# Feed-forward output products as block products: 7 of 256 columns in place of 8, with sums on VectorE and the residual in DRAM

## The chip, the cores and the metric

One NeuronCore of a Trainium2 chip runs the whole program. The metric is the device time of one execution in microseconds. The kernel is written in a Python tile language: a scheduler orders the instructions of each engine when the program is built, and each engine then works through its own queue in that order and waits on semaphores. PE is TensorE, PEld its weight loads, DVE is VectorE, ACT is ScalarE, POOL is GpSimd, and SP issues the weights' DMAs.

## The reference

A trunk of two layers works on a residual x of 512 tokens by 1024 channels, in float32. Each layer is a half feed-forward step, a mixer, and another half feed-forward step:

```
x = x + 0.5 * swiglu(rms_norm(x), w_i1, w_o1)
h = rms_norm(x); p = h @ w_in            # q/k/v of four mixers and the gates' logits
merged = sum_b sigmoid(gate_b) * (branch_b @ w_branch_b)
x = x + merged @ w_out
x = x + 0.5 * swiglu(rms_norm(x), w_i2, w_o2)

def swiglu(h, w_i, w_o):
    gate, up = jnp.split(h @ w_i, 2, axis=-1)
    return (jax.nn.silu(gate) * up) @ w_o
```

The hidden width of the feed-forward networks (FFN) is 2816, which is 22 chunks of 128. There are four FFNs, called a0, b0, a1 and b1 after their place ahead of the mixer or behind it and their layer.

## The kernel before

**Products.** Channels lie on the 128 partitions and the 512 tokens are the columns. A float32 product is made of three matmuls: weights and activations are each held as a rounded part (hi, h) and a remainder (lo, l), and `mm3` (lines 231 to 236) adds hi·h, hi·l and lo·h into one PSUM tile. The weights are the stationary operand, 128x128, loaded anew for each matmul; the activations move, 512 columns at a time.

**Weights.** `load_split` (lines 141 to 152) brings in up to four chunks of 128 columns at once: SP issues a DMA into a raw tile (three buffers), ACT copies it into hi, and DVE (in part of the mixer in turn with POOL) subtracts to get lo. `chain` does that for a row of chunks and issues their mm3.

**An FFN.** In the in stage, for each of 22 j, two chains of eight chunks make a gate and an up-projection; DVE multiplies both by the norm's scale, ACT applies silu, and the product is split into fh and fl, which all stay in SBUF. In the out stage, for each m of eight output rows, one chain of 22 chunks makes a PSUM tile, `L278` adds half of it to the residual x[m], which lies in SBUF, and the next norm squares it, sums the squares (ssq) and makes its parts xh and xl (`L188`, `L189`).

**The mixer.** After four attention branches come, for each branch and each m, a gate (three ACT steps, `L614` to `L616`) and a branch product; DVE multiplies them (`L632`) and adds them to acc[m] (`L634`). Then eight chains over mh and ml, the two parts of acc (`L1087`, `L1088`), make the output product pmo, to which the residual xr is added as it comes back from DRAM. Tiles of mh and ml are taken from rings that the mixer has used for other tiles.

What sets the order on an engine is the scheduler, by the order of the code, the buffers and `high_priority`; the mixer has its own planner, which the change leaves as it is.

Of the kernel before, what the change touches and what calls it, by code (L numbers as in the profile page):

```python
# [21 lines left out]
P = 128  # L22
D = 1024
S = 512
# [24 lines left out]
COL = 64  # L49
RING = 8192  # L50
# [44 lines left out]
def trunk_kernel(ctx: ExitStack, tc: tile.TileContext, a, out):  # L95
# [43 lines left out]
    lo_parts = dict(count=0, shared=False)  # L139

    def load_split(src, n, name):
        raw = wp.tile([P, CW], F32, tag="raw", name=f"raw{name}", bufs=3)
# [23 lines left out]
    class Norm:  # L166
        def __init__(self, l, which, name):
            self.l, self.col, self.name = l, PV[which], name
            self.xh, self.xl = [], []
            self.ssq = per.tile([P, S], F32, tag="ssq", name=f"ssq{name}")  # L170
# [12 lines left out]

        def split(self, m, xt):
            g = pv[:, self.l, self.col + m:self.col + m + 1]
            xh = per.tile([P, S], F32R, tag="xh", name=f"xh{self.name}_{m}", bufs=NK)
            xl = per.tile([P, S], F32R, tag="xl", name=f"xl{self.name}_{m}", bufs=NK)
            A.activation(xh, xt, AF.Copy, scale=g)  # L188
            V.scalar_tensor_tensor(xl, xt, g, xh.bitcast(F32), ALU.mult, ALU.subtract)  # L189
            self.xh.append(xh)  # L190
            self.xl.append(xl)
# [61 lines left out]
    def ffn(l, w_in, w_out, x, nrm, nxt, name, final, early=None):  # L253
        with tc.tile_pool(name=f"ff{name}", bufs=2, reuse_waits="tile") as fp:
            fh, fl = [], []
            for j in range(NH):
                if j == 2 and early is not None:
                    early()
                pg = mm_tile(f"pg{name}{j}")
                chain(pg, w_in[l, j, 0], nrm.xh, nrm.xl, f"g{name}{j}")  # L260
                pu = mm_tile(f"pu{name}{j}")
                chain(pu, w_in[l, j, 1], nrm.xh, nrm.xl, f"u{name}{j}")
                g = fp.tile([P, S], F32, tag="g", name=f"g{name}{j}")
                u = fp.tile([P, S], F32, tag="u", name=f"u{name}{j}")
                V.tensor_tensor(g, pg, nrm.rb, ALU.mult)
                A.activation(g, g, AF.Silu)
                V.tensor_tensor(u, pu, nrm.rb, ALU.mult)
                V.tensor_tensor(u, u, g, ALU.mult)
                h = fp.tile([P, S], F32R, tag="fh", name=f"fh{name}{j}", bufs=NH)
                lo = fp.tile([P, S], F32R, tag="fl", name=f"fl{name}{j}", bufs=NH)  # L270
                A.activation(h, u, AF.Copy)
                V.tensor_tensor(lo, u, h.bitcast(F32), ALU.subtract)
                fh.append(h)
                fl.append(lo)
            for m in range(NK):
                po = mm_tile(f"po{name}{m}")
                chain(po, w_out[l, m], fh, fl, f"o{name}{m}")
                V.scalar_tensor_tensor(x[m], po, 0.5, x[m], ALU.mult, ALU.add)  # L278
                if final:
                    (nc.sync if m == NK - 1 else nc.gpsimd).dma_start(out[m], x[m])  # L280
                else:
                    nxt.add(m, x[m], lambda n: fp.tile([P, S], F32, tag="sq", name=n, bufs=2))
# [54 lines left out]
    def mixer(l, x, nrm, nxt, xs):  # L337
        with (tc.tile_pool(name=f"mx{l}", bufs=1, reuse_waits="tile") as mp,
# [260 lines left out]
            acc = []  # L599
            wbr = {}  # L600

            def gate(b, m):
# [3 lines left out]
                if b == 0:  # L606
                    g = per.tile([P, S], F32, tag="x", name=f"acc{l}{m}", bufs=NK)
# [468 lines left out]


            lo_parts["shared"] = False
# [32 lines left out]
    with tc.tile_pool(name="first", bufs=2) as fp:  # L1111
        with tc.high_priority(offset=2 * HP):
            for m, t in enumerate(x):
                nrm.split(m, t)
# [76 lines left out]
```

## Time and profile before

| | |
|---|---|
| median of 3 runs | 2689.72 us (2689.0 to 2690.22) |
| the profiled execution's own time | 2689.76 us |
| its span | 2688.0 us |
| PE busy | 2669.4 us, 99% of the span |
| DVE, ACT, POOL busy | 55%, 49%, 12% |
| out stage of each FFN | 119.80 us |

The median is what a change is measured by. The span is what the trace covers of the profiled execution, from its first to its last instruction. The busy shares are averages over stages that differ. The out stages are the four windows from the first output matmul of an FFN to its last.

### The profile page before, as it was taken

Reading aid. Unit: us, or ns where it says so; the run is one execution under the profiler, and the core shown is the slowest. Engines: PE = TensorE matmul, PEld = TensorE weight load, DVE = VectorE, ACT = ScalarE, POOL = GpSimd, SP = SyncE. Lnnn points to the kernel's source line nnn. Section 1 sums busy time; section 2 is a strip of 40 time slices with the busy share of each in tenths; the row PEclk is TensorE's granted clock in tenths of the full one; section 3 lists DMA queues with packets and bytes.
Section 4 is the critical chain, followed back from the end, with each engine's and each line's share of the span. In section 5 each row is a group of like instructions: output and inputs, shape, how many; then the busy total and the mean of one; then the engine's idle time right before and its main releaser. Section 6 shows DMA issues by size and latency. Waiting matters only on the chain.

```text
span 2688.0 us, 36812 instructions
## 1 busy us (share of the span) xinstructions
PE 2669.4 (99%) x13054; PEld 2266.4 (84%) x13054; DVE 1486.0 (55%) x3028; ACT 1326.1 (49%) x2740; POOL 318.9 (12%) x438
## 2 busy tenths in 40 slices
PE   9999999999999999999999999999999999999999
PEld 7888889888888788888888888998888887888887
DVE  6444437777764564444354443487776646644432
ACT  4333347777665653333333333477776556433321
POOL 1000012222222200000000000222222222000000
PEclk9999999999999999999999999999999999999999
DMA  5333432222322332233322233322223223322233
GB/s 169 99 98 93 118 117 73 75 72 88 88 76 81 101 114 97 96 98 95 98 98 96 97 101 112 113 69 78 76 84 92 69 87 106 110 98 98 96 109 90
DMA packets 146488, 257.10 MB, mean 96 GB/s; under 512 B 17081, under 2 KB 47801, under 8 KB 146304
## 3 DMA queue, kind: packets, MB, share of 16 engines
q1 hardware_dynamic: 138960, 233.16, 28.1%
q0 software_dynamic: 6192, 19.50, 2.5%
q8 instruction: 102, 1.67, 0.3%
q10 hardware_dynamic: 1152, 2.10, 0.2%
q14 instruction: 82, 0.67, 0.1%
HBM read 248.31 MB, written 8.61 MB: 96 GB/s over the span
## 4 chain that ended last, share of the span: by engine, by line
PE 97%; DVE 1%; ACT 1%; issue 1%; DMA 0%; POOL 0%; ACTq 0%; POOLq 0%
PE pgl L234 4%; PE pgl L236 4%; PE pgl L235 4%; PE pga L235 3%; PE pua L234 3%; PE pua L236 3%; PE pua L235 3%; PE pga L236 3%; PE pga L234 3%; PE pob L236 3%; PE pub L234 3%; PE pgb L234 3%; PE pub L236 3%; PE poa L236 3%; PE pgb L236 3%; PE poa L235 3%
## 5 line engine op out<-in xcount | busy, mean ns | idle before, releaser
L234 PE MATMUL pgl<-xhm,higl 128*128 128x512 f32 x512 | 216.4, 423 | 0.0
L236 PE MATMUL pgl<-xhm,logl 128*128 128x512 f32 x512 | 200.9, 392 | 0.0
L235 PE MATMUL pgl<-xlm,higl 128*128 128x512 f32 x512 | 200.2, 391 | 0.0
L234 PE MATMUL pga<-xhf,higa 128*128 128x512 f32 x352 | 138.1, 392 | 3.0 <-ACT xhf L188 3.0
L150 DVE TENSOR_TENSOR loob<-rawob,hiob 128x512 fp32r<-128x512 f32 x96 | 62.0, 646 | 140.6 <-ACT hiob L147 140.6
L234 PE MATMUL pua<-xhf,hiua 128*128 128x512 f32 x352 | 137.9, 392 | 0.0
L235 PE MATMUL pga<-xlf,higa 128*128 128x512 f32 x352 | 137.4, 391 | 0.4 <-DVE xlf L189 0.4
L147 ACT ACTIVATE hiob<-rawob 128x512 fp32r<-128x512 f32 x96 | 57.3, 597 | 163.2 <-PE pob L235 138.3
L234 PE MATMUL pgb<-xhf,higb 128*128 128x512 f32 x352 | 137.8, 391 | 0.0
L235 PE MATMUL pua<-xlf,hiua 128*128 128x512 f32 x352 | 137.5, 391 | 0.0
L236 PE MATMUL pga<-xhf,loga 128*128 128x512 f32 x352 | 137.4, 390 | 0.0
L236 PE MATMUL pua<-xhf,loua 128*128 128x512 f32 x352 | 137.4, 390 | 0.0
L235 PE MATMUL pub<-xlf,hiub 128*128 128x512 f32 x352 | 137.0, 389 | 0.0
L234 PE MATMUL pub<-xhf,hiub 128*128 128x512 f32 x352 | 137.0, 389 | 0.0
L235 PE MATMUL pgb<-xlf,higb 128*128 128x512 f32 x352 | 137.0, 389 | 0.0
L236 PE MATMUL pub<-xhf,loub 128*128 128x512 f32 x352 | 137.0, 389 | 0.0
L235 PE MATMUL pob<-flb,hiob 128*128 128x512 f32 x352 | 136.9, 389 | 0.0
L234 PE MATMUL pob<-fhb,hiob 128*128 128x512 f32 x352 | 136.9, 389 | 0.0
L234 PE MATMUL poa<-fha,hioa 128*128 128x512 f32 x352 | 136.9, 389 | 0.0
L236 PE MATMUL poa<-fha,looa 128*128 128x512 f32 x352 | 136.9, 389 | 0.0
L236 PE MATMUL pgb<-xhf,logb 128*128 128x512 f32 x352 | 136.9, 389 | 0.0
L235 PE MATMUL poa<-fla,hioa 128*128 128x512 f32 x352 | 136.9, 389 | 0.0
(663 smaller groups left out, 7371.1 us busy)
## 6 DMA issues: line engine op xcount, KB each, us to landing
rawgl<-in_w_gate SPq DMA_DIRECT2D x128, 256.0 KB, 2.7
rawga<-in_f_in SPq DMA_DIRECT2D x88, 256.0 KB, 2.7
rawua<-in_f_in SPq DMA_DIRECT2D x88, 256.0 KB, 2.8
rawgb<-in_f_in SPq DMA_DIRECT2D x88, 256.0 KB, 2.7
rawub<-in_f_in SPq DMA_DIRECT2D x88, 256.0 KB, 2.8
rawoa<-in_f_out SPq DMA_DIRECT2D x80, 256.0 KB, 2.6
rawob<-in_f_out SPq DMA_DIRECT2D x80, 256.0 KB, 2.6
rawmo<-in_w_out SPq DMA_DIRECT2D x32, 256.0 KB, 2.8
```

What stands on the lines that cost most here:

```text
L147: A.activation(hi[:, :n], raw[:, :n], AF.Copy)
L150: eng.tensor_tensor(lo[:, :n], raw[:, :n], hi[:, :n].bitcast(F32), ALU.subtract)
L234: T.matmul(ps, wh, xh, start=first, stop=False)
L235: T.matmul(ps, wh, xl, start=False, stop=False)
L236: T.matmul(ps, wl, xh, start=False, stop=last)
```

## The change

In the out stage of an FFN, the chunks are divided into plain ones (14 in a0, 8 in the other three) and pairs (4 in a0, 7 in the others; `NPAIRS`). The eight output rows are taken two at a time (four `Pair`s q). The plain chunks keep their chains of 512 columns. For a pair of rows, a pair of chunks and the two halves of the columns there are four weight blocks (a, b of the first row, c, d of the second) and four blocks of activations, whose eight block products of 256 columns are replaced by seven:

- `combine`, at the end of the in stage, makes four blocks of sums and differences of activations on DVE, and splits the seven blocks that are used into fph and fpl;
- `group` handles up to four pairs of chunks at a time (four and three where there are seven): it loads the weights a, c, d and b (512 or 384 columns each), makes four sums of them on DVE (`plus`: c+d, a+c+d, a+c, a+b+c+d), splits the seven, and issues the seven products a, s, t, b, u, v, d, each into 256 columns of its own PSUM bank;
- `after` adds the seven PSUM tiles into the two rows of the residual, once the last group is done;
- the weights of w_out lie in DRAM in an order that suits these loads.

The residual isn't kept in SBUF any more: it is loaded on POOL's queue where it is needed (`x_of`) and stored there when it is new (`keep`). The parts of a norm, xh and xl, get a pool of their own, opened and closed around their use. The mixer's last part is a function of its own, `merge`, with a pool that is opened behind the mixer's; its eight mh and ml tiles come from there. The raw weights have four buffers in place of three. The making of the bias tables (`early`, in a0 alone) moves from the third j of the in stage to the second Pair of the out stage. The core of the diff:

```diff
+NPAIRS = (4, 7)
+TH = S // 2
+SLOT = dict(a=0, s=5, t=4, b=2, u=1, v=3, d=6)
...
-        raw = wp.tile([P, CW], F32, tag="raw", name=f"raw{name}", bufs=3)
+        raw = wp.tile([P, CW], F32, tag="raw", name=f"raw{name}", bufs=4)
...
+    def ffn(l, w_in, w_out, x_of, nrm, nxt, name, keep, early=None):
+        with tc.tile_pool(name=f"ff{name}", bufs=1, reuse_waits="tile") as fp:
+            plain, paired = [], []
+            npair = NPAIRS[early is None]
+            nplain = NH - 2 * npair
...
+                r2 = ip.tile([P, S], F32, tag="r", name=f"r{nm}")
+                r3 = ip.tile([P, TH], F32, tag="rs", name=f"rs{nm}")
+                V.tensor_tensor(r2[:, lo], r0[:, lo], r0[:, hi], ALU.subtract)
+                V.tensor_tensor(r2[:, hi], r1[:, hi], r2[:, lo], ALU.add)
+                V.tensor_tensor(r3, r1[:, lo], r2[:, hi], ALU.subtract)
+                V.tensor_tensor(r0[:, hi], r0[:, hi], r1[:, hi], ALU.subtract)
+                h = fp.tile([P, 7 * TH], F32R, tag="fph", name=f"fph{nm}", bufs=npair)
+                lw = fp.tile([P, 7 * TH], F32R, tag="fpl", name=f"fpl{nm}", bufs=npair)
+                for n, r in enumerate((r0, r1, r2, r3)):
+                    c = slice(n * S, n * S + (S if n < 3 else TH))
+                    split_up(h[:, c], lw[:, c], r)
+                paired.append((h, lw))
...
+                    elif j % 2 == 0:
+                        before = u
+                    else:
+                        combine(j // 2, before, u, ip)
+            nrm.close()
...
+                            xr = op.tile([P, S], F32, tag="x", name=f"x{name}{m}", bufs=4)
+                            nc.gpsimd.dma_start(xr, x_of[m])
+                            po = mm_tile(f"po{name}{m}")
+                            chain(po, w_out[l, m][:, :nplain * P], [h for h, _ in plain], [w for _, w in plain],
+                                  f"o{name}{m}")
+                            V.scalar_tensor_tensor(xr, po, 0.5, xr, ALU.mult, ALU.add)
+                            self.x.append(xr)
...
+                        def load(n, m, odd):
+                            if n == "b":
+                                t = op.tile([P, CW], F32, tag="wb", name=f"w{n}{nm}")
+                            else:
+                                t = wp.tile([P, CW], F32, tag="raw", name=f"w{n}{nm}", bufs=4)
+                            nc.sync.dma_start(t[:, :w], w_out[l, 2 * self.q + m][:, c0 + odd * w:c0 + (odd + 1) * w])
+                            return t[:, :w]
...
+                            t = op.tile([P, CW], F32, tag="ws", name=f"s{n}{nm}", bufs=3)[:, :w]
+                            with tc.high_priority(offset=HP):
+                                V.tensor_tensor(t, x, y, ALU.add)
...
+                            sl = slice(SLOT[n] * TH, (SLOT[n] + 1) * TH)
+                            for p in range(np_):
+                                fh, fl = paired[p0 + p]
+                                mm3(ps, hi, lo, p, fh[:, sl], fl[:, sl], p0 + p == 0, p0 + p == npair - 1)
+                            if last:
+                                self.after(n)
+                        a11 = load("a", 0, 0)
+                        a21 = load("c", 1, 0)
+                        product("a", a11)
+                        a22 = load("d", 1, 1)
+                        s1 = plus(1, a21, a22)
+                        s2 = plus(2, s1, a11)
+                        product("s", s2)
+                        product("t", s1)
+                        a12 = load("b", 0, 1)
+                        s3 = plus(3, a11, a21)
+                        product("b", a12)
+                        s4 = plus(4, s2, a12)
+                        product("u", s3)
+                        product("v", s4)
+                        product("d", a22)
...
+                        if n == "a":
+                            self.y = op.tile([P, S], F32, tag="y", name=f"y{nm}")
+                            A.activation(self.y[:, lo], ps, AF.Copy, scale=0.5)
+                        elif n == "s":
+                            self.up = op.tile([P, TH], F32, tag="up", name=f"up{nm}")
+                            V.scalar_tensor_tensor(self.up, ps, -0.5, self.y[:, lo], ALU.mult, ALU.add)
+                        elif n == "t":
+                            V.scalar_tensor_tensor(self.y[:, hi], ps, 0.5, self.up, ALU.mult, ALU.add)
+                            V.tensor_tensor(x1, x1, self.y, ALU.add)
+                        elif n == "b":
+                            V.scalar_tensor_tensor(x1[:, lo], ps, 0.5, x1[:, lo], ALU.mult, ALU.add)
+                        elif n == "u":
+                            self.z = op.tile([P, S], F32, tag="y", name=f"z{nm}")
+                            V.scalar_tensor_tensor(self.z[:, lo], ps, 0.5, self.up, ALU.mult, ALU.subtract)
+                            V.scalar_tensor_tensor(self.z[:, hi], self.ps["t"], -0.5, self.z[:, lo], ALU.mult, ALU.add)
+                            V.tensor_tensor(x2, x2, self.z, ALU.add)
+                        elif n == "v":
+                            V.scalar_tensor_tensor(x1[:, hi], ps, 0.5, x1[:, hi], ALU.mult, ALU.add)
+                            self.out(0)
+                        else:
+                            V.scalar_tensor_tensor(x2[:, lo], ps, 0.5, x2[:, lo], ALU.mult, ALU.add)
+                            self.out(1)
...
+                        (nc.sync if nxt is None and m == NK - 1 else nc.gpsimd).dma_start(keep[m], self.x[n])
+                        if nxt is not None:
+                            nxt.add(m, self.x[n], lambda nm: op.tile([P, S], F32, tag="sq", name=nm))
...
+                for q in range(NK // 2):
+                    if q == 1 and early is not None:
+                        early()
+                    t = Pair(q)
+                    for p0 in range(0, npair, 4):
+                        t.group(p0, min(4, npair - p0), p0 + 4 >= npair)
...
+    def merge(l, acc, nxt, xs, keep):
+        with tc.tile_pool(name=f"mo{l}", bufs=1, reuse_waits="tile") as mp:
             lo_parts["shared"] = False
             mh, ml = [], []
             for m in range(NK):
-                if m < 7:
-                    h = mp.tile([P, S], F32R, tag="oh", name=f"mh{l}{m}", bufs=7)
-                    lo = mp.tile([P, S], F32R, tag="ol", name=f"ml{l}{m}", bufs=7)
-                else:
-                    h = mp.tile([P, S], F32R, tag="st", name=f"mh{l}{m}", bufs=12)
-                    lo = mp.tile([P, S], F32R, tag="st", name=f"ml{l}{m}", bufs=12)
+                h = mp.tile([P, S], F32R, tag="mh", name=f"mh{l}{m}", bufs=NK)
+                lo = mp.tile([P, S], F32R, tag="ml", name=f"ml{l}{m}", bufs=NK)
                 A.activation(h, acc[m], AF.Copy)
                 V.tensor_tensor(lo, acc[m], h.bitcast(F32), ALU.subtract)
                 mh.append(h)
                 ml.append(lo)
-            xn = []
             for m in range(NK):
-                xr = sb_tile(f"xr{l}{m}")
+                xr = mp.tile([P, S], F32, tag="xr", name=f"xr{l}{m}", bufs=3)
                 nc.gpsimd.dma_start(xr, xs[m])
                 po = mm_tile(f"pmo{l}{m}")
                 chain(po, a["w_out"][l, m], mh, ml, f"mo{l}{m}")
-                t = per.tile([P, S], F32, tag="x", name=f"xn{l}{m}", bufs=NK)
+                t = mp.tile([P, S], F32, tag="xn", name=f"xn{l}{m}", bufs=5)
                 V.tensor_tensor(t, po, xr, ALU.add)
+                nc.gpsimd.dma_start(keep[m], t)
+                nxt.add(m, t, lambda nm: mp.tile([P, S], F32, tag="r", name=nm, bufs=6))
...
+            mixer(l, nrm, ap, acc)
+            nrm.close()
+            nxt.open()
+            merge(l, acc, nxt, xs, x)
```

On the engines the rows of the mixer, up to its last gate, stand as before; each engine has the rows of the out stages anew. PE has 13482 rows where it had 12582, which is 900 more: 3 x 252 for the three FFNs with 7 pairs and 144 for a0.

ACT at the end of layer 0's mixer, before. himo is the hi part of the weights of the output product, gt037 the gate of the last branch and row, mh05 to mh07 the copies of acc:

```order
L147 ACTIVATE himo01_0_10004<-rawmo01_0_10002 128x512
L147 ACTIVATE himo01_4_10022<-rawmo01_4_10020 128x512
L1087 ACTIVATE mh06_9945<-acc06_6134 128x512
L614 ACTIVATE gt037_9909<-gt037_9909,pv_101 128x512
L615 ACTIVATE gt037_9909<-gt037_9909,onec_94 128x512
L147 ACTIVATE himo02_0_10052<-rawmo02_0_10050 128x512
L616 ACTIVATE gt037_9909<-gt037_9909 128x512
L1087 ACTIVATE mh07_9949<-acc07_6235 128x512
L147 ACTIVATE himo02_4_10070<-rawmo02_4_10068 128x512
```

The same place after the change:

```order
L151 ACTIVATE himo01_0_10392<-rawmo01_0_10390 128x512
L151 ACTIVATE himo01_4_10410<-rawmo01_4_10408 128x512
L759 ACTIVATE gt037_10286<-gt037_10286,pv_101 128x512
L760 ACTIVATE gt037_10286<-gt037_10286,onec_94 128x512
L761 ACTIVATE gt037_10286<-gt037_10286 128x512
L1230 ACTIVATE mh00_10308<-acc00_5481 128x512
L1230 ACTIVATE mh01_10312<-acc01_5558 128x512
L1230 ACTIVATE mh02_10316<-acc02_5713 128x512
L1230 ACTIVATE mh03_10320<-acc03_5835 128x512
L1230 ACTIVATE mh04_10324<-acc04_5947 128x512
```

mh00 to mh05 stood earlier, in turn with the gates before; now all eight stand together behind the third step of gt037.

DVE at the same place after the change. pbr037 is the last branch product, ml00 and on the remainders of acc:

```order
L154 TENSOR_TENSOR lomo01_0_10393<-rawmo01_0_10390,himo01_0_10392 128x512
L154 TENSOR_TENSOR lomo01_4_10411<-rawmo01_4_10408,himo01_4_10410 128x512
L777 TENSOR_TENSOR gt037_10286<-pbr037_10291,gt037_10286 128x512
L779 TENSOR_TENSOR acc07_6612<-acc07_6612,gt037_10286 128x512
L1231 TENSOR_TENSOR ml00_10309<-acc00_5481,mh00_10308 128x512
L1231 TENSOR_TENSOR ml01_10313<-acc01_5558,mh01_10312 128x512
```

Before, ml00 to ml05 stood earlier in the same way as mh00 to mh05; now all eight stand behind the operation that finishes acc07.

PE at the same place, before and then after:

```order
L234 MATMUL pbr037_9914<-oh0D_9646,hibr034_9766 128x512
L235 MATMUL pbr037_9914<-ol0D_9647,hibr034_9766 128x512
L236 MATMUL pbr037_9914<-oh0D_9646,lobr034_9767 128x512
L234 MATMUL pmo00_9955<-mh00_9921,himo00_0_9958 128x512
L235 MATMUL pmo00_9955<-ml00_9922,himo00_0_9958 128x512
L236 MATMUL pmo00_9955<-mh00_9921,lomo00_0_9959 128x512
```

```order
L249 MATMUL pbr037_10291<-oh0D_10023,hibr034_10143 128x512
L250 MATMUL pbr037_10291<-ol0D_10024,hibr034_10143 128x512
L251 MATMUL pbr037_10291<-oh0D_10023,lobr034_10144 128x512
L249 MATMUL pmo00_10342<-mh00_10308,himo00_0_10345 128x512
L249 MATMUL pmo01_10389<-mh00_10308,himo01_0_10392 128x512
L250 MATMUL pmo00_10342<-ml00_10309,himo00_0_10345 128x512
L251 MATMUL pmo00_10342<-mh00_10308,lomo00_0_10346 128x512
L249 MATMUL pmo00_10342<-mh01_10312,himo00_0_10345 128x512
```

Nothing stands between the last branch product and the first matmul of pmo in either; after the change the chains of pmo00 and pmo01 take turns.

DVE in the out stage of b0 after the change, second Pair, where the first group (name b01_0) and the second (b01_4) meet. s1 to s4 are the sums of weights, lo with a letter the remainder of a product's weights, pob02 and pob03 the plain chains of the two rows:

```order
L355 TENSOR_TENSOR s3b01_0_13156<-wab01_0_13093,wcb01_0_13095 128x512
L336 SCALAR_TENSOR_TENSOR xb02_13013<-pob02_13015,xb02_13013 128x512
L276 TENSOR_TENSOR losb01_0_13121<-s2b01_0_13118,hisb01_0_13120 128x512
L276 TENSOR_TENSOR lotb01_0_13138<-s1b01_0_13116,hitb01_0_13137 128x512
L355 TENSOR_TENSOR s4b01_0_13175<-s2b01_0_13118,wbb01_0_13154 128x512
L355 TENSOR_TENSOR s1b01_4_13249<-wcb01_4_13230,wdb01_4_13247 128x384
L336 SCALAR_TENSOR_TENSOR xb03_13053<-pob03_13055,xb03_13053 128x512
L276 TENSOR_TENSOR lobb01_0_13159<-wbb01_0_13154,hibb01_0_13158 128x512
L276 TENSOR_TENSOR loub01_0_13178<-s3b01_0_13156,hiub01_0_13177 128x512
L355 TENSOR_TENSOR s2b01_4_13251<-s1b01_4_13249,wab01_4_13228 128x384
L276 TENSOR_TENSOR lovb01_0_13195<-s4b01_0_13175,hivb01_0_13194 128x512
L355 TENSOR_TENSOR s3b01_4_13285<-wab01_4_13228,wcb01_4_13230 128x384
```

The second group's first sum, s1b01_4, stands ahead of the split of product b of the first group. Before, this stretch of DVE held two weight splits for each four chunks of a plain chain and nothing else.

## Rows read from the trace of the kernel before

**Rows 1.** The page: busy time by engine; the chain that ended last
```profile
PE 2669.4 (99%) x13054; PEld 2266.4 (84%) x13054; DVE 1486.0 (55%) x3028; ACT 1326.1 (49%) x2740; POOL 318.9 (12%) x438
...
PE 97%; DVE 1%; ACT 1%; issue 1%; DMA 0%; POOL 0%; ACTq 0%; POOLq 0%
```

**Rows 2.** Busy time by window, the second output stage, below the view's columns
```profile
core 0: us, PE busy (x) PEld busy (x) DVE busy (x) ACT busy (x) POOL busy (x), PEclk, DMA share, GB/s
...
1229.80:1349.60 119.80, 119.80 (x530) 99.25 (x529) 46.06 (x71) 38.16 (x64) 0.00 (x0) 1.00 0.34 96
```

**Rows 3.** Timeline of PE, end of group D's projection (start us, us)
```profile
2161.53 0.36 PE L362 MATMUL pt1d<-hit1d,xhm 128*128 128x256 f32 x1
2161.73 0.28 PE L363 MATMUL pt1d<-lot1d,xhm 128*128 128x256 f32 x1
...
2161.98 0.28 PE L362 MATMUL pt1d<-hit1d,xhm 128*128 128x256 f32 x1
...
2164.37 0.28 PE L364 MATMUL pt1d<-hit1d,xlm 128*128 128x256 f32 x1
```

**Rows 4.** Single tiles (duration ns min/median/max); two rows of DVE's timeline
```profile
L150 DVE TENSOR_TENSOR looa<-rawoa,hioa x96: 424/691/694, 247.7 to 1700.3; 128x512 fp32r<-128x512 f32 x80, 128x256 fp32r<-128x256 f32 x16
...
L150 DVE TENSOR_TENSOR lot0a<-rawt0a,hit0a x16: 542/557/956, 371.3 to 443.5; 128x384 fp32r<-128x384 f32 x16
...
1405.54 0.68 DVE L150 TENSOR_TENSOR loua<-rawua,hiua 128x512 fp32r<-128x512 f32 x1
1406.14 0.68 DVE L268 TENSOR_TENSOR ua<-ua,ga 128x512 f32<-128x512 f32 x1
```

**Rows 5.** Timeline, the end; DMA issues (KB each, us to landing)
```profile
2684.16 0.69 DVE L278 SCALAR_TENSOR_TENSOR xn<-pob,xn 128x512 f32<-128x512 f32 x1 [8.87 <-PE pob L236]
...
rawoa<-in_f_out SPq DMA_DIRECT2D x80, 256.0 KB, 2.6
```

**Rows 6.** Timeline of PE, the last branch matmul and the first of pmo
```profile
945.73 0.39 PE L236 MATMUL pbr<-oh0D,lobr 128*128 128x512 f32 x1
945.96 0.39 PE L234 MATMUL pmo<-mh,himo 128*128 128x512 f32 x1
```

**Rows 7.** Timeline of ACT around the end of the mixer of layer 0
```profile
945.25 1.31 ACT L147 ACTIVATE himo<-rawmo 128x512 fp32r<-128x512 f32 x2 [2.04 <-PE pgl L235]
946.47 0.62 ACT L1087 ACTIVATE mh<-acc 128x512 fp32r<-128x512 f32 x1
946.99 0.71 ACT L614 ACTIVATE gt<-gt,pv 128x512 f32<-128x512 f32 x1
947.73 0.72 ACT L615 ACTIVATE gt<-gt,onec 128x512 f32<-128x512 f32 x1
...
949.19 0.62 ACT L616 ACTIVATE gt<-gt 128x512 f32<-128x512 f32 x1
```

**Rows 8.** Timeline of DVE there: the last gate's product and sum
```profile
949.93 0.68 DVE L632 TENSOR_TENSOR gt<-pbr,gt 128x512 f32<-128x512 f32 x1
950.64 0.69 DVE L634 TENSOR_TENSOR acc<-acc,gt 128x512 f32<-128x512 f32 x1
```

**Rows 9.** Timeline of PE at the start, and two windows (columns as above)
```profile
8.42 0.80 PE L234 MATMUL pga<-xhf,higa 128*128 128x512 f32 x1 [3.04 <-ACT xhf L188]
...
8.42:14.06 5.64, 5.23 (x12) 3.76 (x12) 5.64 (x12) 5.53 (x10) 0.00 (x0) 0.50 0.95 334
14.06:16.00 1.94, 1.94 (x10) 1.59 (x9) 1.94 (x4) 1.94 (x5) 0.00 (x0) 0.96 0.47 182
```

**Rows 10.** Two shorter idle times of PE, and the windows around them
```profile
461.62 0.63 PE L585 MATMUL pot0A<-ident,o0A 128*128 128x128 f32 x4 [1.42 <-DVE o0A L734]
...
912.28 0.51 PE L234 MATMUL pbr<-oh0D,hibr 128*128 128x512 f32 x1 [1.18 <-ACT oh0D L986]
...
459.00:462.50 3.50, 2.08 (x13) 1.58 (x12) 3.43 (x9) 3.05 (x10) 2.15 (x3) 1.00 0.21 56
909.00:915.00 6.00, 4.19 (x20) 3.05 (x19) 3.20 (x5) 3.55 (x5) 0.78 (x1) 1.00 0.28 89
```

More of the change, by code (lines that the diff above doesn't have):

```diff
@@ L169, in __init__, with open, close @@
             self.xh, self.xl = [], []
-            self.ssq = per.tile([P, S], F32, tag="ssq", name=f"ssq{name}")
+        def open(self):
+            self.pool = tc.tile_pool(name=f"x{self.name}", bufs=1, side="right", reuse_waits="tile")
+            self.xp = self.pool.__enter__()
+            self.ssq = per.tile([P, S], F32, tag="ssq", name=f"ssq{self.name}")
+        def close(self):
+            self.pool.__exit__(None, None, None)
         def add(self, m, xt, alloc):
@@ L250, in chain @@
             pass
[L253 to L280, printed above, removed]
-                else:
-                    nxt.add(m, x[m], lambda n: fp.tile([P, S], F32, tag="sq", name=n, bufs=2))
@@ L1112, in trunk_kernel @@
         with tc.high_priority(offset=2 * HP):
-            for m, t in enumerate(x):
-                nrm.split(m, t)
-        for m, t in enumerate(x):
-            nrm.square(m, t, lambda n: fp.tile([P, S], F32, tag="sq", name=n))
+            for m in range(NK):
+                nrm.split(m, x[m])
+        for m in range(NK):
+            nrm.square(m, x[m], first)
     nrm.finish()
+    x = [a["x"][m] for m in range(NK)]
     for l in range(L):
+        xs = kept(f"xs{l}")
         nxt = Norm(l, "nm", f"m_{l}")
-        ffn(l, a["f1_in"], a["f1_out"], x, nrm, nxt, f"a{l}", False, setup_bias if l == 0 else None)
+        ffn(l, a["f1_in"], a["f1_out"], x, nrm, nxt, f"a{l}", xs, setup_bias if l == 0 else None)
@@ L1121, in trunk_kernel @@
         nxt.finish_cols()
-        xs = [drm.tile([P, S], F32, name=f"xs{l}{m}") for m in range(NK)]
-        for m in range(NK):
-            nc.gpsimd.dma_start(xs[m], x[m])
         nrm, nxt = nxt, Norm(l, "n2", f"f2_{l}")
-        x = mixer(l, x, nrm, nxt, xs)
+        x = kept(f"xt{l}")
+        with tc.tile_pool(name=f"acc{l}", bufs=1, reuse_waits="tile") as ap:
+            acc = []
+            mixer(l, nrm, ap, acc)
+            nrm.close()
+            nxt.open()
+            merge(l, acc, nxt, xs, x)
@@ L1130, in trunk_kernel @@
         nxt = None if last else Norm(l + 1, "n1", f"f1_{l + 1}")
-        ffn(l, a["f2_in"], a["f2_out"], x, nrm, nxt, f"b{l}", last)
+        keep = out if last else kept(f"xu{l}")
+        ffn(l, a["f2_in"], a["f2_out"], x, nrm, nxt, f"b{l}", keep)
+        x = keep
         if not last:
@@ L1139, in _tiles, with _out_order @@
     return w.reshape(l, k // P, P, n // P, P).transpose(0, 3, 2, 1, 4).reshape(l, n // P, P, k)
+def _out_order(npair):
+    first = NH - 2 * npair
+    order = list(range(first))
+    for p0 in range(0, npair, 4):
+        for odd in range(2):
+            order += [first + 2 * p + odd for p in range(p0, min(p0 + 4, npair))]
+    return order
 def _layout(i):
```

94 lines of the change are left out of this document (75 added, 19 removed).

## The prediction

> **What bounds the kernel now.** The page comes first: TensorE (PE) is busy for 99% of the span, VectorE (DVE) for 55%, and 97% of the chain of work that ended last is PE [rows 1]. So time is won by giving PE less to do, and lost where PE has to wait; work on DVE, ScalarE (ACT) or a queue costs nothing until PE waits for it. Next come the windows of the four output stages, 255.20 to 375.00, 1229.80 to 1349.60, 1589.70 to 1709.50 and 2564.30 to 2684.10. The second stands for them [rows 2]: PE is busy for all of its 119.80 us at a granted clock of 1.00, DVE for 46.06 and ACT for 38.16 (the last stage, without a norm behind it, has less of both). A stage is 8 x 22 x 3 = 528 matmuls of 512 columns, so one takes 119.80 / 528 = 0.2269 us from start to start. Its duration in the rows, 0.39, overlaps that of the next.
>
> **What the stage saves.** Per FFN with 7 pairs, 14 of 22 chunks leave the plain chains: 14 x 8 x 3 = 336 matmuls of 512 columns. In comes 4 (pairs of output rows) x 7 (products) x 7 (pairs of chunks) x 3 = 588 of 256. The first FFN (a0) changes 192 into 336. What does one of 256 columns cost, with its own weights each time? The projections of group D show it: from the matmul at 2161.98 to the one at 2164.37 lie 20 intervals of the same form, 2.39 / 20 = 0.1195 us each [rows 3]. New hi and lo tiles come in there every twelve matmuls, as in a product of four pairs.
> - an FFN of 7 pairs: 336 x 0.2269 - 588 x 0.1195 = 76.2 - 70.3 = 6.0 us; three of them 17.9
> - a0: 192 x 0.2269 - 336 x 0.1195 = 43.6 - 40.2 = 3.4 us
> - together **21.3 us**. It breaks even where 256 columns cost 336/588 = 0.571 of 512, which is 0.1297 us: 10 ns above the row.
>
> The rows stand against a rule here. The Trainium skill, "TensorE: Matmul & The Clock Gate", section "Back-to-back issue gap", says that in a stream of weight loads and matmuls the spacing is set by both, with 81 ns at 128 columns and 131 ns at 512; a straight line between gives an estimate of 98 ns at 256, three quarters of the 512, and the change would then lose 588 x 0.098 - 336 x 0.131 = 13.4 us per FFN, some 48 in all. The formula in that section for a lone matmul (N / 2.4 + 2.5 ns, so 215.8 and 109.2) would save 8.3 per FFN and 29.6 in all. Neither pair of figures is met by the rows (226.9 and 119.5), and the sum goes by these.
>
> **What the other engines must do for it.** One pair of output rows with 7 pairs of chunks is 48 matmuls of 512 and 147 of 256, 10.9 + 17.6 = 28.5 us of PE. On DVE it is 21 operations on 512 columns (four weight splits and two evictions of the plain chains, four sums and seven splits of the first group, two sums into x, two of the norm), 11 on 384, 7 on 256 and two norm splits. With the durations 0.69, 0.56 and 0.42 [rows 4], and 0.75 for a norm split taken a little above the 512 row, this is 14.5 + 6.2 + 2.9 + 1.5 = 25.1 us; operations that follow each other start 0.60 apart (1405.54 to 1406.14) where each lasts 0.68, which makes it about 22. That is 77 to 88% of PE's 28.5. ACT copies 512 columns in 0.62 (the mh of [rows 7]) and has some 22 such operations or shorter ones, under half. So neither becomes the bound, but DVE's margin is small, and its queue is in order: a sum that waits for its load holds up the splits behind it.
>
> I followed the queue by these durations. The tightest place is the second group's first sum: its weights can be loaded only when the first group's third sum has freed a raw buffer, and a 256 KB load takes 2.6 us to land [rows 5]. The sum comes four DVE operations later, so it waits some tenths. The split behind it is that of product b, which PE needs only after products a, s and t (3 x 12 x 0.1195 = 4.3 us); about 3 us are left. At the stage's start, the last pair of chunks is combined and split within some twelve DVE operations (under 8 us) of the last up-projection, and the first product comes after 48 matmuls of plain chains, 10.9 us. At its end, the last norm split is a handful of ACT and DVE operations (4 to 5.5 us) behind the last product, and wanted after seven eighths of the next stage's first two chains, 42 x 0.2269 = 9.5 us. I put all of this at nothing. If the cover goes, each microsecond by which a pair is late costs 4 x 3 = 12 us over the three FFNs. The residual's loads and stores are issued on POOL's queue while that engine has 12% of work [rows 1], a pair ahead of their use: nothing. At the very end the last DVE operation on 512 columns (0.69 at 2684.16, [rows 5]) becomes one on 256: -0.3. The table bias work of layer 0 (setup_bias) moves from the in stage to the out stage of a0, which has the lighter load of DVE (4 pairs, not 7): nothing.
>
> **What the split of the mixer costs.** This is the one place where PE gets a new wait. Before, six of the eight copies mh and their remainders ml stood earlier in the queues of ACT and DVE, among the last gates, and PE went from the last branch matmul into the first of pmo at 945.96 with no idle time [rows 6]. Now all eight mh stand behind the last gate's third ACT step, and all eight ml behind the product and the sum that finish acc07 (the lists in the section on the change). PE's first pmo matmul needs mh00, its third ml00. By the rows of before for the same operations [rows 7, 8]:
> - ACT: the two himo splits from 945.25 last 1.31 and end at 946.56. The three gate steps start 0.74 apart (946.99 and 947.73), so without the mh and the himo that stood between them they run at about 946.5, 947.2 and 948.0 and end at 948.6. mh00 (0.62) ends at about 949.2.
> - PE: idle from 945.96 to 949.2, **3.3 us**. It then does two matmuls (pmo00 and pmo01 with mh00), 0.45.
> - DVE: gate times branch can start when ACT's third step is done, 948.6, the sum 0.71 later (949.93 to 950.64), ml00 after it at about 950.0, done at 950.7. PE waits another **1.0 us**.
>
> Behind that an ml is ready every 0.61 us and wanted every 0.68 or more: no further wait. So 4.25 us a layer, 8.5 for two. Below: if the gate steps start sooner and nothing else changes, 3.3 each, 6.6. Above: with the himo splits still between, as in before, one ACT operation more (0.52 in the queue), 9.5.
>
> **The clock.** A wait may cost more than itself. At the start PE sat idle for 3.04 us before 8.42; from there to 14.06 the granted clock was 0.50, which is the lower of the two levels, 1.2 GHz, and these 5.64 us lost half their work, 2.8 us; the 1.94 us behind them, at 0.96, lost another 0.1 [rows 9]. Idle times of 1.42 us (before 461.62) and 1.18 (before 912.28) left it at 1.00 [rows 10]. The new wait of 3.3 us is nearest to the 3.04 that was followed by the low level, so I take 2.9 for each layer, **5.8 us**; bounds 0 and 2 x 2.9.
>
> **The sum**, against the profiled execution's own 2689.76 (which is its span of 2688.0 and 1.76 around it, and within 0.1 of the median of the runs shown): 2689.76 - 21.3 + 8.5 + 5.8 - 0.3 = **2682.5 us**. A change under 0.2% of this time, 5.4 us, can't be told from none.
>
> **The rivals.**
> 1. The clock holds through the new waits: 2689.76 - 21.3 + 8.5 - 0.3 = 2676.7. For it: [rows 10]; against it: [rows 9], with an idle time of the same length. Chance 0.17.
> 2. PE doesn't wait at the merge, because ACT or DVE get through the gate sooner than by the rows: 2689.76 - 21.3 - 0.3 = 2668.2. The order leaves little room: mh00 stands behind the gate's third step in any case. Chance 0.05.
> 3. The other side: the small matmuls cost more than 0.1195. The first matmul behind two short ones of another kind (2161.53) has its follower 0.20 later, at 2161.73 [rows 3]. If the first of each product, which changes weights' tile, operand and bank at once, takes 0.20, then 3 x 56 + 28 = 196 products pay 0.08 each, 15.7 us: 2698.2, slower. It decides from 7.3 / 196 = 0.037 us a product for no gain, and from 0.065 for a loss that can be measured. Against it: the twelve-matmul cadence of [rows 3] runs through a change of tiles without a step, and so do the chains of [rows 2]. Chance 0.10.
> The rule of the section "Back-to-back issue gap" in the Trainium skill is that rival taken to its end; its figures would give about 2738, and since the spacing of rows 3 is already that of loads and matmuls in one stream, I give it 0.01.
> 4. DVE late in the out stages by up to 1 us a pair, at the second group's sum: 2682.5 + 12 = 2694.5, no difference that can be told; from 1.06 us a pair, slower. For it: 77 to 88% of PE's time in an in-order queue; against it: the 3 us of slack. Chance 0.17.
>
> **How the numbers follow.** The forecast has what is left, 0.50; its own range is 2679 to 2687 (0.8 of a microsecond of wait each way per layer, and the bounds of the merge). Faster by over 0.2% is under 2684.4: two thirds of the forecast (0.33), rivals 1 and 2 (0.22), a little of rival 4 (0.04): 0.59. Slower, over 2695.1: most of rival 3 with the rule (0.09) and the worse third of rival 4 (0.06): 0.15. Same: 0.26. The range from 2674 to 2696 leaves out rival 2, most of rival 3 and the tail of rival 4, under 2 in 10.
>
> **What would show it.** In the profile after: out stages of about 113.8 us (116.4 in a0) with PE busy throughout and block matmuls 0.12 apart; DVE at 80% or so in them; one idle time of about 3.3 us and one of about 1 us before pmo in each layer, the first put down to mh's copy and the second to ml's; and behind the first some 5 us at a granted clock of 0.50. The prediction is wrong if the products' matmuls stand over 0.123 apart, if PE shows idle time between products, or if the merge's wait is absent.

## The result and the profile after

The change makes the kernel slower: 2721.94 us median (2719.81 to 2724.02, 4 runs) against 2689.36 us before (2688.91 to 2690.22, 4 runs), a ratio of 1.012 with a 95% interval of 1.0108 to 1.0132, some 32 us. The forecast was 2682.5. The profiled execution after took 2719.81 us with a span of 2718.0.

The page of the kernel after, busy time by engine and the chain that ended last, answers to [rows 1]:

```profile
PE 2691.2 (99%) x13954; PEld 2296.0 (84%) x13954; DVE 1716.1 (63%) x3518; ACT 1396.4 (51%) x2890; POOL 348.4 (13%) x494
...
PE 97%; DVE 2%; ACT 1%; issue 0%; DMA 0%; POOL 0%; DVEq 0%; POOLq 0%
```

PE is still busy for 99% of the span and makes up 97% of the chain, and of the 30.0 us that the span has gained, 21.8 are busy time of PE (2691.2 - 2669.4): it does its work more slowly, or more of it. Windows by stage say where. First b0's in stage before, then its in stage and its out stage after (columns as in [rows 2], which shows the out stage before):

```profile
989.48:1229.74 240.26, 240.26 (x1059) 198.64 (x1058) 117.26 (x177) 86.79 (x136) 0.00 (x0) 1.00 0.30 97
```

```profile
1003.90:1251.16 247.26, 247.26 (x1059) 198.59 (x1058) 130.98 (x213) 90.96 (x147) 1.08 (x2) 1.00 0.31 96
1251.16:1365.34 114.18, 114.18 (x782) 106.58 (x781) 92.04 (x165) 52.41 (x92) 7.02 (x13) 1.00 0.41 128
```

The out stage does what was forecast: 114.18 us from its first matmul to the first of the next stage, where before it was 119.68 ([rows 2] has a window a little wider), with PE busy throughout and DVE for 92.04 us, 81%. The 1056 matmuls of the in stage have the same shapes, the same tiles and the same order as before, and the same granted clock of 1.00; but the stage takes 247.26 us in place of 240.26. That is 0.2342 us for a matmul in place of 0.2275, four times over: no term of the prediction stands for it. PE's timeline within that stage after the change, from one product of three matmuls to the next:

```profile
1099.96 0.39 PE L249 MATMUL pub<-xhf,hiub 128*128 128x512 f32 x1
1100.19 0.40 PE L250 MATMUL pub<-xlf,hiub 128*128 128x512 f32 x1
1100.43 0.39 PE L251 MATMUL pub<-xhf,loub 128*128 128x512 f32 x1
1100.66 0.39 PE L249 MATMUL pub<-xhf,hiub 128*128 128x512 f32 x1
```

There is no idle time between them. The step from hi·xh to hi·xl takes 0.23 us, from hi·xl to lo·xh 0.24, and so on through the stage, without scatter. What waits for nothing and is slower in every instance is slower in itself.

In the out stage, the block matmuls stand 0.12 us apart, as [rows 3] had it: 17 intervals from 1273.24 to 1275.28 make 2.04 / 17 = 0.120.

```profile
1273.24 0.28 PE L249 MATMUL psb<-fphb,hisb 128*128 128x256 f32 x1
...
1275.28 0.28 PE L251 MATMUL ptb<-fphb,lotb 128*128 128x256 f32 x1
```

At the merge of layer 0, PE, ACT and DVE answer to [rows 6], [rows 7] and [rows 8]; then the windows from the first pmo matmul on (PEclk is the third number from the end):

```profile
953.59 0.39 PE L251 MATMUL pbr<-oh0D,lobr 128*128 128x512 f32 x1
957.01 1.22 PE L249 MATMUL pmo<-mh,himo 128*128 128x512 f32 x2 [3.04 <-ACT mh L1230]
958.55 0.80 PE L250 MATMUL pmo<-ml,himo 128*128 128x512 f32 x1 [0.32 <-DVE ml L1231]
...
955.81 0.63 ACT L761 ACTIVATE gt<-gt 128x512 f32<-128x512 f32 x1
956.35 4.26 ACT L1230 ACTIVATE mh<-acc 128x512 fp32r<-128x512 f32 x8
...
957.20 0.69 DVE L779 TENSOR_TENSOR acc<-acc,gt 128x512 f32<-128x512 f32 x1
957.81 4.90 DVE L1231 TENSOR_TENSOR ml<-acc,mh 128x512 fp32r<-128x512 f32 x8
```

```profile
957.00:960.00 3.00, 2.67 (x6) 1.66 (x6) 2.97 (x6) 3.00 (x7) 0.00 (x0) 0.50 0.13 48
960.00:963.00 3.00, 3.00 (x9) 2.33 (x8) 2.71 (x5) 0.60 (x2) 0.00 (x0) 0.50 0.02 5
963.00:970.00 7.00, 7.00 (x32) 5.81 (x31) 2.64 (x4) 2.44 (x5) 0.28 (x1) 0.99 0.23 75
```

PE is idle for 3.04 us until the first mh, then for 0.32 until the first ml, and the clock is at 0.50 until about 963: what the prediction said of this place.

### The profile page after: what moved, and what is told of

The parts are those of the page before. It is cut to its first block, busy times and chain, and to the rows that moved or that the text cites. A ratio compares the mean times of both kernels' runs of the same rounds, so it can differ in the third digit from the quotient of the medians.

```text
span 2718.0 us, 39563 instructions
## 1 busy us (share of the span) xinstructions
PE 2691.2 (99%) x13954; PEld 2296.0 (84%) x13954; DVE 1716.1 (63%) x3518; ACT 1396.4 (51%) x2890; POOL 348.4 (13%) x494
## 4 chain that ended last, share of the span: by engine, by line
PE 97%; DVE 2%; ACT 1%; issue 0%; DMA 0%; POOL 0%; DVEq 0%; POOLq 0%
PE pgl L249 5%; PE pgl L250 4%; PE pgl L251 4%; PE pub L250 3%; PE pub L249 3%; PE pub L251 3%; PE pua L251 3%; PE pua L249 3%; PE pua L250 3%; PE pgb L250 3%; PE pga L251 3%; PE pga L249 3%; PE pga L250 3%; PE pgb L249 3%; PE pgb L251 3%; PE pbr L249 2%
## 5 line engine op out<-in xcount | busy, mean ns | idle before, releaser
L151 ACT ACTIVATE hiub<-rawub 128x512 fp32r<-128x512 f32 x88 | 55.6, 632 | 145.0 <-PE pub L250 139.5
L151 ACT ACTIVATE hiua<-rawua 128x512 fp32r<-128x512 f32 x88 | 55.5, 632 | 141.7 <-PE pua L250 133.8
L154 POOL TENSOR_TENSOR logl<-rawgl,higl 128x512 fp32r<-128x512 f32 x64 | 83.0, 1296 | 258.7 <-ACT higl L151 229.1
L251 PEld LDWEIGHTS pgl<-xhm,logl 128*128 128x128 f32 x512 | 96.2, 188 | 23.1
L249 PEld LDWEIGHTS pgl<-xhm,higl 128*128 128x128 f32 x512 | 97.1, 190 | 17.1
L154 DVE TENSOR_TENSOR loub<-rawub,hiub 128x512 fp32r<-128x512 f32 x88 | 60.4, 687 | 79.1 <-ACT hiub L151 79.1
L151 ACT ACTIVATE higl<-rawgl 128x512 fp32r<-128x512 f32 x128 | 80.6, 630 | 57.0 <-PE pgl L250 38.5
```

The costliest lines, as they stand in the source:

```text
L151: A.activation(hi[:, :n], raw[:, :n], AF.Copy)
L154: eng.tensor_tensor(lo[:, :n], raw[:, :n], hi[:, :n].bitcast(F32), ALU.subtract)
L249: T.matmul(ps, wh, xh, start=first, stop=False)
L251: T.matmul(ps, wl, xh, start=False, stop=last)
```

## The experiments

The tiles' addresses in SBUF are fixed when the program is built. Before, all xh and xl begin at a multiple of 128 bytes (the first at 30336). After, the new pool lies against the upper end of SBUF, and all sixteen begin 32 bytes beyond a multiple of 64 (the first at 196576). That gave **theory A**, that a matmul takes longer where its moving operand starts off such a boundary. Its rivals were B, that the place at the top of SBUF does it, and C, that other engines' new work in the in stage slows PE.

| kernel | median, us | kernel before | ratio (95% interval) |
|---|---|---|---|
| the change | 2721.94 | 2689.36 | 1.012 (1.0108 to 1.0132) |
| e1_aligned | 2701.37 | 2689.75 | 1.0046 (1.0029 to 1.0063) |
| e2_before_plus32 | 2722.02 | 2689.75 | 1.0122 (1.0107 to 1.0137) |
| e3_merge_back | 2686.75 | 2689.75 | 0.9994 (0.9984 to 1.0003) |
| e4_no_pairs | 2717.33 | 2689.75 | 1.0103 (1.0088 to 1.0118) |
| e5_offsets | 2715.05 | 2689.73 | 1.0096 (1.0082 to 1.011) |
| e6_filler | 2694.40 | 2689.73 | 1.0018 (1.0009 to 1.0027) |
| e7_aligned128_merge_back | 2674.08 | 2689.73 | 0.9944 (0.9932 to 0.9957) |
| e8_weights_plus32 | 2743.63 | 2689.73 | 1.0201 (1.0185 to 1.0216) |
| e9_aligned128 | 2686.49 | 2689.42 | 0.9988 (0.9978 to 0.9997) |

**e1_aligned** shifts xh and xl by 32 bytes:

```diff
+    top = ctx.enter_context(tc.tile_pool(name="top", bufs=1, side="right"))
+    pad = top.tile([P, 8], F32, name="pad")
...
+    V.memset(pad, 0.0)
```

> The changed kernel with one 32-byte tile ahead of the right-hand pool, so that xh and xl start at a multiple of 64 bytes (before 32 beyond one), still at the top of SBUF. Theory A (matmuls whose 512 moving columns start off a 64-byte boundary take longer): in stages of b0, a1, b1 go from 247.0 us back to 240.0, that of a0 loses about as much, pgl matmuls from 0.232 to 0.227; 4 x 7.0 + 2 x 3.3 = 35 us less, about 2687. Theory B (it is the place at the top of SBUF): no change, 2722, in stages 247. Theory C (more work of VectorE or DMA in the in stage slows TensorE): no change either, 2722.

The window of b0's in stage:

```profile
998.25:1240.84 242.59, 242.59 (x1059) 198.70 (x1058) 130.66 (x213) 91.07 (x147) 1.08 (x2) 1.00 0.32 98
```

242.59 us: 4.7 of the 7.0 us are back, and with them 20.6 us of the whole. A shift of 32 bytes at the same place, with the same work around it, does that, so B and C fall. But theory A expected all 7.0 back, and 2687. The new start, 196544, is a multiple of 64 and not of 128.

**e2_before_plus32** does the reverse in the kernel before:

```diff
             self.ssq = per.tile([P, S], F32, tag="ssq", name=f"ssq{name}")
+            if name == "f1_0":
+                V.memset(per.tile([P, 8], F32, tag="pad0", name="pad0"), 0.0)
...
+            if self.name == "f1_0":
+                V.memset(per.tile([P, 8], F32, tag="pad1", name="pad1"), 0.0)
```

> The kernel before, with 32 bytes put ahead of xh and 32 behind xl, so that these sixteen tiles alone start 32 bytes beyond a multiple of 64; they stay at the low addresses, and nothing else changes. Theory A: each in stage 240.0 to 247.0, gates 3.3 us a layer, so 2689.4 + 35 = about 2724. Theories B and C: 2689, in stages 240.0.

```profile
998.49:1245.74 247.25, 247.25 (x1059) 198.77 (x1058) 118.67 (x177) 87.13 (x136) 0.00 (x0) 1.00 0.29 94
```

The in stage is 247.25, as after the change, and the whole is 32.3 us longer, about what the change cost. The kernel before contains no block product, no merge of its own and no residual in DRAM.

The two pads move more than the expectation says, though. Everything that lies behind them starts 64 bytes later, the weights' tiles hi and lo and all fh and fl among it (in the program as built the first hi goes from 71552, a multiple of 128, to 71616, and the first fh from 96128 to 96192). So in e2's in stage the moving operand starts 32 bytes beyond a multiple of 128 and the weights 64; in its out stage both start 64 beyond one. That out stage of b0, which took 119.68 us before from its first matmul to the first of the next stage:

```profile
1245.74:1365.44 119.70, 119.70 (x529) 99.10 (x528) 46.10 (x71) 38.02 (x64) 0.00 (x0) 1.00 0.34 96
```

Both operands off by the same 64 bytes cost nothing there.

**e3_merge_back** adds to e1 the mixer's last part as it was before the change:

```diff
-    def mixer(l, nrm, ap, acc):
+    def mixer(l, nrm, ap, acc, nxt, xs, keep):
...
+                if m < 7:
+                    h = mp.tile([P, S], F32R, tag="oh", name=f"mh{l}{m}", bufs=7)
+                    lo = mp.tile([P, S], F32R, tag="ol", name=f"ml{l}{m}", bufs=7)
+                else:
+                    h = mp.tile([P, S], F32R, tag="st", name=f"mh{l}{m}", bufs=12)
+                    lo = mp.tile([P, S], F32R, tag="st", name=f"ml{l}{m}", bufs=12)
...
+            nrm.close()
+            nxt.open()
...
-            merge(l, acc, nxt, xs, x)
```

> The aligned version of the changed kernel, with the mixer's last part put back inside the mixer (mh and ml from its rings, as before the change). If the wait at the merge and the low clock behind it cost what the trace of the changed kernel shows (3.0 us idle, then pmo chains 3.4 to 3.9 us longer, two layers: 13 us): no idle time before pmo, clock 1.00 there, 13 us less than the aligned version, about 2674, faster than the kernel before by some 15 us. Rival (the wait is only moved to the next stage): equal to the aligned version within 2 us.

14.6 us less than e1: the merge's wait isn't moved to another place, it goes. The total misses 2674 by 12.8 us, because that figure took e1 to reach 2687 and e1 had stopped 14.4 above it.

**e4_no_pairs** is e1 with `NPAIRS = (0, 0)` and the two rows stored without products:

```diff
-NPAIRS = (4, 7)
+NPAIRS = (0, 0)
...
+                    if not npair:
+                        t.out(0)
+                        t.out(1)
```

> The aligned version of the changed kernel with no block products at all: 22 plain chunks in every FFN, all else as in the change (residual in DRAM, separate merge). If the block products save what the out stages show (119.45 to 114.05 us in three FFNs, half of it in the first: 19 us): 19 us more than the aligned version, out stages of 119.5. If the sums cost elsewhere what the products save: equal to the aligned version.

Its out stage of b0:

```profile
1243.62:1363.33 119.71, 119.71 (x530) 99.10 (x529) 46.10 (x71) 38.03 (x64) 7.03 (x13) 1.00 0.43 126
```

119.71 us against 114.16 in e1, and 16.0 us more in all, 3 less than expected (the two profiled executions, 2717.35 and 2698.31, lie 19.0 apart): the products do save time, and their sums cost nothing elsewhere that would undo it.

**e5_offsets** gives each stage another start, in the kernel before:

```diff
+OFFS = {"f1_0": (1, 1), "m_0": (4, 4), "f2_0": (16, 16), "f1_1": (8, 0), "m_1": (16, 16), "f2_1": (0, 8)}
...
+            oh, ol = OFFS[self.name]
+            xh = per.tile([P, S + 32], F32R, tag="xh", name=f"xh{self.name}_{m}", bufs=NK)[:, oh:oh + S]
+            xl = per.tile([P, S + 32], F32R, tag="xl", name=f"xl{self.name}_{m}", bufs=NK)[:, ol:ol + S]
```

> The kernel before, with xh and xl as slices of wider tiles whose bases are multiples of 128 bytes; the start of a slice differs by stage: a0 both 4 bytes on, b0 both 64, a1 xh alone 32, b1 xl alone 32; mixer of layer 0 both 16, of layer 1 both 64. In stages of before: 246.5, 240.0, 240.0, 240.0. Theory D (a start that is no multiple of 128 bytes costs, one at 64 less than any other): a0 about 253.5, b0 about 242.4 as in the stages of the aligned version, a1 and b1 between 240 and 247 and together +7, total about 2713. Rival E (only multiples of 64 count, and the 2.3 us left in each in stage of the aligned version have another cause): b0 240.0, the rest the same, total about 2709. Rival F (32 bytes is a special case, shorter offsets cost nothing): a0 246.5.

The in stages of a0 (4 bytes), b0 (64), a1 (32, xh alone) and b1 (32, xl alone):

```profile
8.24:265.96 257.72, 257.02 (x1064) 202.14 (x1065) 130.49 (x204) 95.18 (x152) 6.81 (x13) 0.99 0.34 108
1001.84:1245.63 243.79, 243.79 (x1060) 198.74 (x1058) 117.86 (x177) 87.22 (x136) 0.00 (x0) 1.00 0.29 95
1365.33:1610.25 244.92, 244.92 (x1059) 198.56 (x1058) 118.06 (x177) 87.31 (x136) 0.00 (x0) 1.00 0.29 95
2345.49:2589.27 243.78, 243.78 (x1059) 198.53 (x1058) 117.95 (x177) 87.57 (x136) 0.00 (x0) 1.00 0.30 95
```

64 bytes cost 3.5 us (243.79 to 240.26), so E falls: xh and xl at a multiple of 64 that is none of 128 lose time against weights at a multiple of 128. D had put that at 2.4, as in e1; why the same 64 bytes cost 2.3 there and 3.5 here isn't shown. Even 4 bytes cost, 11 us in a0 (from its first matmul to its last, 246.53 before and 257.49 now), so F falls; theory D had put that at 7. xh and xl each bear a part, 4.7 and 3.5, together 8.2 where D had 7. And e2's out stage goes against D as it is worded: a start that is no multiple of 128 cost nothing where both operands had the same one.

**e6_filler** puts work without use into the wait of e1's merge:

```diff
+                junk = s_tile(f"junk{l}")
+                for _ in range(13):
+                    T.matmul(junk, nrm.xh[0][:, :P], nrm.xh[1], start=True, stop=True)
```

> The aligned version with the separate merge, and 13 matmuls without use, on xh, between the last branch product and the first of pmo in each layer, about the length of the wait. If the low clock behind the wait is caused by the idle time: clock 1.00 in the pmo chains, pmo chains of 43.6 us in place of 45.5 and 46.8, 4 to 6 us less than the aligned version, about 2696. If the clock falls for another reason, or the pmo chains are longer for want of ml: equal to the aligned version, 2701, or later by what the 13 matmuls overrun.

PE's timeline there, and the window that follows:

```profile
948.05 3.13 PE L1228 MATMUL junk<-xhm,xhm 128*128 128x512 f32 x13
951.26 0.73 PE L253 MATMUL pmo<-mh,himo 128*128 128x512 f32 x2
952.79 0.50 PE L254 MATMUL pmo<-ml,himo 128*128 128x512 f32 x1 [0.80 <-DVE ml L1239]
```

```profile
954.30:960.00 5.70, 5.70 (x27) 4.72 (x26) 4.02 (x7) 1.81 (x4) 0.00 (x0) 1.00 0.04 11
```

The clock stays at 1.00. The two profiled executions differ by 4.2 us (2698.31 and 2694.12), of which some 1.5 belong to another fall of the clock in e1's, of the kind described at the end; the medians differ by 7.0, where 4 to 6 were expected, and what makes up the rest of that isn't shown. The wait for the first ml, 0.80 us, stays. With PE at work in place of the wait the clock doesn't fall, so it is the idle time that makes it fall, and a wait of 3 us costs about twice its length.

**e7_aligned128_merge_back** is e3 with 96 bytes of padding in place of 32:

```diff
-    pad = top.tile([P, 8], F32, name="pad")
+    pad = top.tile([P, 24], F32, name="pad")
```

> The version with the merge put back, its 32 bytes of padding made 96, so that xh and xl start at a multiple of 128 bytes. Theory D: in stages of 240.0 in place of 242.4 to 243.3, gate stages 1.4 us a layer shorter, 10 to 12 us less, about 2675, faster than the kernel before by 14 to 15 us (0.5%). Rival E: no change, 2686.8, the same as the kernel before.

Its in stage and out stage of b1, and PE at the merge of layer 0:

```profile
2312.69:2552.96 240.27, 240.27 (x1060) 198.64 (x1059) 130.80 (x214) 90.67 (x147) 1.08 (x2) 1.00 0.33 102
2552.96:2667.20 114.24, 114.24 (x781) 106.54 (x779) 85.93 (x153) 43.70 (x77) 7.30 (x14) 1.00 0.39 118
```

```profile
944.08 0.39 PE L255 MATMUL pbr<-oh0D,lobr 128*128 128x512 f32 x1
944.30 0.39 PE L253 MATMUL pmo<-mh,himo 128*128 128x512 f32 x1
```

240.27 is the time of before, the out stage has kept its gain, and PE goes from the last branch product into pmo without idle time. 2674.08 us is 0.56% under the kernel before: this version beats both.

**e8_weights_plus32** shifts the other operand, in the kernel before:

```diff
-        hi = wp.tile([P, CW], F32R, tag="hi", name=f"hi{name}")
-        lo = wp.tile([P, CW], F32R, tag="lo", name=f"lo{name}")
+        hi = wp.tile([P, CW + 32], F32R, tag="hi", name=f"hi{name}")[:, 8:8 + CW]
+        lo = wp.tile([P, CW + 32], F32R, tag="lo", name=f"lo{name}")[:, 8:8 + CW]
```

> The kernel before, with the weights' tiles hi and lo 32 bytes beyond a multiple of 128, xh and xl unmoved. If only the moving operand's start matters: 2689.7, all stages as before. If the stationary operand's start matters as much: every stage longer, by up to 5 ns a matmul, 40 to 60 us more.

In stage and out stage of b1:

```profile
2367.36:2614.61 247.25, 247.25 (x1059) 198.68 (x1058) 118.69 (x177) 87.37 (x136) 0.00 (x0) 1.00 0.29 94
2614.61:2737.80 123.19, 123.19 (x529) 98.96 (x527) 35.09 (x55) 27.42 (x46) 3.79 (x7) 1.00 0.34 98
```

The stationary operand's start matters as much: (247.25 - 240.26) / 1056 = 6.6 ns a matmul in the in stage, and in the out stage, from first matmul to last, 122.97 us in place of 119.45, 3.52 / 528 = 6.7; 53.9 us in all, since every product with weights reads them from these tiles.

The runs so far fit one reading: the two operands' starts count against each other, not each by itself. Take the moving operand's start less the weights', modulo 128. It is 96 in the change (96 and 0), in e2's in stage (32 and 64) and here (0 and 32), and all three in stages of b0 or b1 take 247.25 to 247.26 us; it is 0 in the kernel before (0 and 0) and in e2's out stage (64 and 64), which is as fast. If each start had its own price, both stages of e2 should pay for two. No run was made to test this reading; one with both operands moved by the same 32 bytes would.

**e9_aligned128** is the change with the 96 bytes of padding and nothing else (the edits of e1 and e7 to `pad`):

> The changed kernel with 96 bytes of padding ahead of the right-hand pool and nothing else, so that xh and xl start at a multiple of 128 bytes; the merge stays a function of its own. Theory D with the merge as priced by the traces so far: in stages of 240.0, the wait and low clock at the merge stay (6.4 to 6.9 us a layer), so 2674.1 + 13 = about 2687, 33 to 35 us less than the changed kernel, and the same as the kernel before within 0.2%. If the gain of the version with the merge put back came from the interplay of both edits: above 2692.

Its in stage of b0, and 3 us within the pmo chains of layer 0:

```profile
995.36:1235.62 240.26, 240.26 (x1059) 198.58 (x1058) 130.64 (x213) 91.05 (x147) 1.08 (x2) 1.00 0.33 99
...
950.84:953.84 3.00, 3.00 (x9) 2.32 (x8) 2.69 (x5) 0.60 (x2) 0.00 (x0) 0.50 0.03 5
```

2686.49, as expected: 96 bytes ahead of a pool are worth 35.5 us, and the low clock at the merge is still there. It is faster than the kernel before by 0.12%, just clear of none (the interval ends at 0.9997).

## Why the prediction was wrong

**The step that failed** is the one that isn't there. Under "What the split of the mixer costs" the prediction says "This is the one place where PE gets a new wait", and the sum takes for granted that every matmul that the change doesn't rewrite costs what it did. That xh and xl get a pool of their own stands in the section on the change; the prediction gave it no term. It moved the moving operands of 4 x 1056 matmuls of the in stages, and of the gates', from a multiple of 128 bytes to 32 beyond one of 64, while their weights stayed at multiples of 128. No wait shows it and no instruction is added. The runs price it at 2721.94 - 2686.49 = 35.5 us (the change against e9), and the reverse edit at 32.3 (e2).

The Trainium skill's page "SBUF — State Buffer", section "Operand start alignment", wants an operand's start at a multiple of its element size and says that it speaks of legality and not of speed. The starts after the change satisfy it; e2, e5 and e8 show the speed.

The other terms, by the traces of before, after and e9:

| term | forecast | measured |
|---|---|---|
| block products, three FFNs | -17.9 | -16.3: 119.45 to 114.01 us from first to last matmul of b0's and b1's out stage, a1's alike |
| a0 | -3.4 | -1.0: in stage 1.75 shorter, out stage 0.75 longer (e9), the bias matmuls having moved from one to the other |
| wait and clock at the merge, two layers | +8.5 +5.8 | +12.4 (e9 against e7) |
| start of xh and xl | none | +35.5 |

- Right: 256 columns with own weights cost 0.120 us, and no first matmul of a product stood out, so rival 3 did not come. The estimate of 98 ns at 256 columns, worked out from the figures in the Trainium skill, "TensorE: Matmul & The Clock Gate", section "Back-to-back issue gap", isn't met by the trace. The term was mis-sized by 1.6 us of 17.9, since 512 columns cost 0.2267 from start to start, less than 0.2269, and 256 slightly more than 0.1195.
- Right: DVE at 81% in the out stage held nothing up; PE shows no idle time there, so rival 4 did not come. Nor did rivals 1 and 2: PE did wait, and the clock did fall.
- Right: the wait at the merge, its two parts and its causes. 3.04 us was the first part (3.3 forecast), 0.32 in layer 0 and 0.63 in layer 1 the second (1.0), and the clock fell, as [rows 9] suggested and [rows 10] did not.
- Forecast 2.4 us too high: the saving of a0. Moving the bias tables was costed at nothing. The six matmuls that moved take 2.8 us, so the in stage should have been 2.8 shorter and was 1.75; in the profile after, PE waits there for DVE's ga for 0.63 us, a new wait that the prediction didn't have. Without the six, the out stage is some 2 us shorter in place of 3.4; what takes the rest isn't shown.
- By the measured terms the change costs 35.5 + 12.4 - 16.3 - 1.0 = 30.6 us. The spans differ by 30.0, the medians by 32.6; the runs after lie up to 4 us apart, and what sets that apart is not settled. A part of it may be what follows below.

## What to carry to other kernels

Where a change moves tiles, look up where both operands of a matmul start, as one would count the instructions that it adds: here xh and xl at no multiple of 128 bytes, with weights at one, cost each fp32 matmul of 512 columns some 2 to 10 ns (2.3 us in 1056 in e1, 11.0 in a0 of e5), which no wait shows and which the spacing of matmuls in a stage that wasn't touched gives away. Compare the stages that a change does not rewrite before those that it does. And look where the first writers of a new pool come to stand in the queues: here a pool opened behind the mixer's end put all mh and ml behind the last gate, which made two waits of 3 us, doubled by the clock.

## What the hardware showed unexpectedly

- Where a matmul's operands start in SBUF sets its pace: +6.6 ns with xh and xl 96 bytes beyond a multiple of 128 and the weights at one (the change), the same with the weights 32 beyond one and xh and xl at one (e8), and nothing with both 64 beyond one (e2's out stage). Why 4 bytes cost more than 64 was not tried further, nor any boundary above 128.
- An idle time of 1.18 us followed by one of 0.61 stands before the last branch products in every run. In [rows 10] the clock held at 1.00 there. In e3 it fell, at the same place in the same instructions; in e7 it held:

```profile
914.54 0.51 PE L253 MATMUL pbr<-oh0D,hibr 128*128 128x512 f32 x1 [1.18 <-ACT oh0D L1135]
915.66 0.65 PE L254 MATMUL pbr<-ol0D,hibr 128*128 128x512 f32 x1 [0.61 <-DVE ol0D L1136]
```

```profile
916.50:919.00 2.50, 2.50 (x7) 2.00 (x6) 1.64 (x3) 0.00 (x0) 0.00 (x0) 0.50 0.00 1
```

```profile
910.64 0.50 PE L253 MATMUL pbr<-oh0D,hibr 128*128 128x512 f32 x1 [1.17 <-ACT oh0D L1135]
911.75 0.50 PE L254 MATMUL pbr<-ol0D,hibr 128*128 128x512 f32 x1 [0.62 <-DVE ol0D L1136]
```

```profile
913.00:916.00 3.00, 3.00 (x15) 2.46 (x14) 3.00 (x6) 0.89 (x2) 0.00 (x0) 1.00 0.00 0
```

So whether a short wait costs its length or more isn't settled by its length; each fall here made seven or eight matmuls take 0.43 us in place of 0.23, some 1.5 us.
